# A fused decoder layer on one core: in the compression, work that one engine hands to another is issued further ahead, and a last column changes engine

## The chip, the cores and the metric

The kernel runs on one core of a Trainium2 chip. A core has five engines with a queue of instructions each: TensorE (matmuls, PE in the profile, its weight loads PEld), VectorE (DVE), ScalarE (ACT), GpSimd (POOL) and SyncE (SP, which here issues most DMA transfers). Each engine takes its instructions in the order in which the program issued them; between engines, semaphores make a reader wait for its writer. The metric is the device time of one execution in microseconds, as a median of several runs.

## The reference, cut to what matters

One decoder layer for 320 tokens (256 of a prompt, 8 x 8 of running requests): a SwiGLU feed-forward, a mixer of retention heads and of sparse attention, and a second feed-forward, each with a residual and a LayerNorm. The change lies in one part of the sparse attention, the compression of the cached keys and values of 8 requests of 2048 tokens:

```
chunks = x.reshape(B, n_chunks, 16, 2, 128)
h = einsum('pd,pdf->f', pos_emb, w1)
for r in range(2):
    h = h + einsum('bnskd,sdf->bnkf', chunks, w1r[r])[:, r:r + n_cmp]
return einsum('bnkf,fd->bnkd', gelu(h), w2)
```

It is done once for the keys and once for the values, each with weights of its own: w1 (4096 x 256) and w2 (256 x 128).

## The kernel before, in words

All products are made in a split form: a float32 operand is written as a high half (a rounded copy, ScalarE, line 219) plus a low half (the difference, VectorE, line 220), and `mm3` (lines 213 to 215) issues three matmuls for one product. `split` issues the two halves; the second of the three matmuls is the first that needs the low half of the moving operand.

A generator-based scheduler decides the order in which instructions are issued. The main generator issues a few matmuls, adds their estimated time to a clock, and yields; then `tick` runs one step of each background task that is due (two steps at most). A task yields the time until its next step, or a condition. The scheduler does not reorder a queue: the order of issue is the order on each engine.

The compression (`compress`) goes over 64 rows m, each in two halves (n = 2m and 2m + 1); 8 rows make a pair (two requests; pairs 0 to 3 are keys, 4 to 7 values). A half row has 18 matmuls in three groups of six, with a tick after each group: two groups use the two parts "e" and "o" of the row's chunks, the third uses their sum ("both") with the sum of the two matching weights ("cs"), so that three products do the work of four. At the start of row m:

- `cx_split(m + 2)` splits e and o of the row after next (ScalarE 128x1024, VectorE 128x1024) and then adds them in place (VectorE, line 716);
- `cx_both(m + 1)` splits that sum for the next row (128x512 on each);
- `cx_load` issues page loads from the cache, six of every eight on SP and two on GpSimd. They go into rooms that rows read before have freed.

The split weights of the keys (`cw`, tag G) and their sums (`cs`, on tags wh, wl, K0 and x0) are replaced part by part (k = 0 to 7) by those of the values while pairs 3 and 4 run: a load on SP, a split (`cw_split`), the sum of the two halves of the table on GpSimd (`cw_sum`, line 668), and the split of that sum (`cs_split`). At the start of the stage the last two key sums (k = 6, 7) are made in the same way.

When a pair is done, a background task `cpost` takes its three accumulators over: it combines them (lines 833 to 839), applies position bias and gelu (lines 844, 845, and 815 to 819 in `gelu`), multiplies with w2 on TensorE (tag cw2), for each half f of the hidden width, and writes the result to DRAM (`c_aside`, line 862). The tiles y and u of its work are in the ring of x that the next stage (`w_in_nsa`) needs: the first high half of x (line 539) lies there.

Of the kernel before, what the change touches and what calls it, by code (L numbers as in the profile page):

```python
# [11 lines left out]
AF = mybir.ActivationFunctionType  # L12
# [155 lines left out]
class Builder:  # L168
# [556 lines left out]
    def compress(self):  # L725

        raw = {}

        loads = {}
        for half, first, n in ((2, 0, 16), (3, 2, 8), (5, 6, 8), (4, 10, 16)) + tuple((h, 4 * h - 10, 8) for h in range(6, 16)):  # L730
            for k in range(32 // n):
                loads.setdefault(first + k, []).append((half, n * k, n * k + n))
        for n in range(128):
            m, s2 = divmod(n, 2)
            pair, i = divmod(m, 8)
            if s2 == 0:
                if n == 0:
                    self.rr_rest()
                if m < 62:
                    self.cx_split(m + 2)  # L740
                if m < 63:
                    self.cx_both(m + 1)
                    self.rows_split = m == 62
                for load in loads.get(m, ()):
                    self.cx_load(*load)
            if n in (3, 5, 7, 9):
                k = n // 2 + 3
                room = self.sums_room(k)
                if k > 5:
                    self.cw_sum(room, self.chunk[:, 1024 * (k % 2):1024 * (k % 2) + 1024])  # L750
                self.cs_split(k, room)
            if n in (32, 40):
                raw[n // 8 - 4] = self.cw_load(1, n // 8 - 4)
            if i == 0 and s2 == 0:

                banks = {6: ("x0", "m0", "m3"), 7: ("x2", "x3", "x1")}
                acc = [self.p(t) for t in banks.get(pair, ("x2", "x3", "m1") if pair % 2 else ("x0", "x1", "m0"))]
                if pair == 7:
                    self.free = ["x0"]
            eo, both = self.cx_ring(m)  # L760
            for t in range(3):
                for f in range(2):
                    if t < 2:
                        o = (2 * s2 + 1 - t) * 256 + 128 * f
                        wh, wl = (self.cw[i][:, k, o:o + 128] for k in range(2))
                        hi, lo = (x[:, 512 * s2 + 256 * t:512 * s2 + 256 * t + 256] for x in eo)
                    else:
                        o = s2 * 256 + 128 * f
                        wh, wl = (self.cs[i][k][:, o:o + 128] for k in range(2))
                        hi, lo = (x[:, 256 * s2:256 * s2 + 256] for x in both)  # L770

                    self.mm3(acc[t][:, 256 * f:256 * f + 256], wh, wl, hi, lo, i == 0 and s2 == 0 and f == 0,
                             i == 7 and s2 == 1 and f == 1, 0.11)
                yield
            k, step = divmod(2 * (n - 50), 7)
            if 0 <= k < 8 and step in (0, 1):

                self.cw_split(k, raw[k])
            elif 0 <= k < 8 and step in (2, 3):

                r = raw.pop(k)
                place = r.rearrange("p (s h f) -> p s h f", s=2, h=2)[:, :, 0]
                self.cw_sum(place, r)
                self.cs_split(k, place)
                if k < 6:
                    raw[k + 2] = self.cw_load(1, k + 2)
            if i == 7 and s2 == 1:
                self.posts += 1
                self.spawn(self.cpost(pair, acc), 0.3 if pair < 7 else 10.0)
            if n == 116:  # L790
                self.w_limit, self.ahead = len(self.wq), 0
                self.w_feed()
            if n == 112:

                self.kh, self.kl = 1, 0
                self.x_back(range(0, 12, 2))
                self.x_back([14], self.chunk[:, 0:640].rearrange("p (k t) -> p k t", k=2))
            elif n == 117:
                self.spawn(self.x_scale())
            elif n in (118, 123):  # L800
                self.ahead += 1
                self.w_feed()
        self.compressed = True
# [5 lines left out]
            self.nc.sync.dma_start(out=d, in_=self.x_aside[:, m:m + 2])  # L809
            self.d[m:m + 2] = d[:, 0], d[:, 1]  # L810

    def gelu(self, hs, u, wait=0.0):

        nc = self.nc
        nc.vector.scalar_tensor_tensor(u, u, 1.0 / 0.044715, hs, op0=ALU.add, op1=ALU.mult)
        yield wait
        nc.scalar.activation(u, u, AF.Tanh, scale=0.044715 * math.sqrt(2.0 / math.pi))
        yield wait
        nc.vector.scalar_tensor_tensor(u, u, 1.0, hs, op0=ALU.add, op1=ALU.mult)

    def cpost(self, pair, acc):

        nc = self.nc
        kind, b = pair // 4, 2 * (pair % 4)
        work = self.work[1] if pair < 7 else self.t([128, 1024], "r0")
        y, u = work[:, 0:512], work[:, 512:1024]
        w2 = self.cw2[kind]
        po = (yield from self.hold()) if pair == 7 else self.p("m2")
        rows = y.rearrange("p (m r v) -> p r m v", r=2, v=2)
        two = lambda a: a.rearrange("p (m v) -> p m v", v=2)  # L830
        for f in range(2):
            q, p, c = (a[:, 256 * f:256 * f + 256] for a in acc)
            nc.scalar.activation(u[:, 0:256], q, AF.Copy)
            yield 1.0
            nc.vector.tensor_tensor(rows[:, 1, 0:127], two(p[:, 0:254]), two(u[:, 2:256]), op=ALU.add)
            nc.scalar.activation(rows[:, 1, 127:128], two(p[:, 254:256]), AF.Copy)
            yield 0.6
            nc.vector.tensor_tensor(u[:, 0:256], p, u[:, 0:256], op=ALU.add)
            nc.vector.tensor_tensor(rows[:, 0], two(c), two(u[:, 0:256]), op=ALU.subtract)
            if pair == 7 and f:  # L840
                self.free += ["x2", "x3", "x1"]
            yield 1.5
            pc = self.posc[:, 2 * kind + f:2 * kind + f + 1]
            nc.scalar.activation(u, y, AF.Square, bias=pc)
            nc.scalar.activation(y, y, AF.Identity, bias=pc)
            yield 1.5
            yield from self.gelu(y, u, 1.5)
            yield 5.0 if pair < 7 else 2.5
            if kind == 0:
                self.mm(po, w2[:, f], u, f == 0, f == 1, 0.86)  # L850
            else:
                for k in range(4):
                    g = u[:, 256 * (k // 2):256 * (k // 2) + 256].rearrange("p (n v) -> p n v", v=2)[:, :, k % 2]
                    self.mm(po[:, 128 * k:128 * k + 128], g, w2[:, f], f == 0 and k == 0, f == 1 and k == 3, 0.22)
        if kind == 0:
            nc.scalar.activation(y.rearrange("p (b v n) -> p b n v", b=2, v=2),
                                 po.rearrange("p (b n v) -> p b n v", b=2, v=2), AF.Copy, scale=0.5)
        else:
            nc.scalar.activation(y, po, AF.Copy, scale=0.5)
        if pair == 7:  # L860
            self.drop(po)
        nc.gpsimd.dma_start(out=self.c_aside[:, kind, 256 * b:256 * b + 512], in_=y)
        self.posts -= 1
        if pair == 7:
            self.kc, self.vc = (self.t([128, 8, 256], f"K{k}") for k in range(2))
            for k, t in enumerate((self.kc, self.vc)):
                nc.gpsimd.dma_start(out=t.rearrange("p b c -> p (b c)"), in_=self.c_aside[:, k])
            self.kc = self.kc.rearrange("p b (v n) -> p b v n", v=2)
# [1022 lines left out]
```

## Time and profile before

| | us |
|---|---|
| median of 3 runs | 2881.12 (2876.95 to 2886.17) |
| profiled execution, its own time | 2884.2 |
| its span, first to last instruction | 2882.5 |
| TensorE busy | 2797.6 (97%) |
| VectorE busy | 1553.5 (54%) |
| ScalarE busy | 1202.3 (42%) |
| GpSimd busy | 346.5 (12%) |

The mean granted TensorE clock is 0.991 of full speed. The compression lies between about 950 and 1271 us of the span. A busy TensorE is not one at its peak: matmuls overlap, their ends are modelled, and a short wait can hide under a drawn end. So matmuls in a stretch are counted as well as waits. In a list of instructions, the bracket gives the engine's idle time before the instruction and what ended it.

### The profile page before, as it was taken

The page shows a single profiled execution, that of the slowest core. Times are in us where ns is not written, and L with a number is a line of the kernel's source. Part 1 is how long each engine was busy: PE and PEld are TensorE (multiplying, and loading weights), DVE is VectorE, ACT ScalarE, POOL GpSimd, SP SyncE. Part 2 cuts the span into 40 slices and gives each one's busy share as a digit, 9 for nine tenths or more (in the row PEclk, how much of TensorE's full clock was granted, in tenths as well). Part 3 has the DMA queues.
Part 4 walks back from the last instruction along what each step waited for, and adds up shares of the span by engine and source line. Part 5 has one row for each costly group of instructions (what it writes and reads, how often), then busy time and mean ns, then how long its engine had stood idle before and what let it go on. Part 6 is the DMA issues. An engine that isn't in the chain of part 4 may idle for free. (4 is left out here: it accounts for less than half of the span.)

```text
span 2882.5 us, 49616 instructions
## 1 busy us (share of the span) xinstructions
PE 2797.6 (97%) x19841; PEld 2715.4 (94%) x19841; DVE 1553.5 (54%) x1921; ACT 1202.3 (42%) x1684; POOL 346.5 (12%) x420
## 2 busy tenths in 40 slices
PE   9999999999999998989999999999999999999996
PEld 9999999999999997988888888989999999999996
DVE  4333333357768667684574455673333333366665
ACT  4333333344445455444444445343333333355453
POOL 0000000000102223213232111350000000001111
PEclk9999999999999999999999999999999999999998
DMA  6555444456657444336667664544444444444442
GB/s 225 177 195 177 153 147 153 147 161 199 198 167 235 133 132 137 116 130 239 196 229 252 227 220 164 194 136 154 152 149 150 150 150 150 149 147 151 147 150 92
DMA packets 202600, 484.74 MB, mean 168 GB/s; under 512 B 24257, under 2 KB 100930, under 8 KB 200450
## 3 DMA queue, kind: packets, MB, share of 16 engines
q1 hardware_dynamic: 192546, 451.30, 48.6%
q0 software_dynamic: 9824, 30.29, 3.1%
q8 instruction: 155, 2.54, 0.4%
q14 instruction: 75, 0.61, 0.1%
HBM read 467.47 MB, written 22.28 MB: 170 GB/s over the span
## 5 line engine op out<-in xcount | busy, mean ns | idle before, releaser
L220 DVE TENSOR_TENSOR wl<-raw,wh 128x1024 fp32r<-128x1024 f32 x650 | 816.2, 1256 | 1082.5 <-ACT wh L219 1062.9
L219 ACT ACTIVATE wh<-raw 128x1024 fp32r<-128x1024 f32 x650 | 688.1, 1059 | 1169.6 <-PE m L214 1130.5
L213 PE MATMUL m<-x,wh 128*128 128x320 f32 x3664 | 1150.5, 314 | 12.3 <-ACT wh L219 6.4
L214 PE MATMUL m<-x,wh 128*128 128x320 f32 x3664 | 1134.5, 310 | 4.6 <-DVE x L540 4.6
L215 PE MATMUL m<-x,wl 128*128 128x320 f32 x3664 | 1133.9, 309 | 0.4 <-DVE wl L220 0.4
L213 PEld LDWEIGHTS m<-x,wh 128*128 128x128 f32 x3664 | 692.0, 189 | 36.1 <-issue 22.6
L214 PEld LDWEIGHTS m<-x,wh 128*128 128x128 f32 x3664 | 692.4, 189 | 6.9 <-DVE x L540 6.2
L215 PEld LDWEIGHTS m<-x,wl 128*128 128x128 f32 x3664 | 691.7, 189 | 0.8 <-DVE wl L220 0.8
L213 PE MATMUL m<-r,wh 128*128 128x320 f32 (+1 forms) x1592 | 495.8, 311 | 3.6 <-ACT r L219 1.8
L214 PE MATMUL m<-r,wh 128*128 128x320 f32 (+1 forms) x1592 | 488.3, 307 | 6.6 <-DVE r L220 6.6
L215 PE MATMUL m<-r,wl 128*128 128x320 f32 (+1 forms) x1592 | 490.8, 308 | 0.0
L213 PEld LDWEIGHTS m<-r,wh 128*128 128x128 f32 x1592 | 299.0, 188 | 9.8 <-issue 3.7
L214 PEld LDWEIGHTS m<-r,wh 128*128 128x128 f32 x1592 | 299.4, 188 | 9.3 <-DVE r L220 8.4
L215 PEld LDWEIGHTS m<-r,wl 128*128 128x128 f32 x1592 | 298.2, 187 | 0.0
L476 POOL TENSOR_TENSOR t<-x,x 128x320 f32<-128x320 f32 x3 | 2.7, 914 | 1415.7 <-DVE x L456 719.9
L220 DVE TENSOR_TENSOR r<-G,r 128x640 fp32r<-128x640 f32 (+1 forms) x184 | 156.7, 856 | 0.0
L213 PE MATMUL x<-r,G 128*128 128x256 f32 x480 | 138.6, 289 | 0.0
L214 PE MATMUL x<-r,G 128*128 128x256 f32 x480 | 136.6, 285 | 0.0
L215 PE MATMUL x<-r,G 128*128 128x256 f32 x480 | 136.4, 284 | 0.0
L219 ACT ACTIVATE r<-G 128x640 fp32r<-128x640 f32 (+1 forms) x184 | 130.1, 712 | 0.0
L220 DVE TENSOR_TENSOR r<-x,r 128x1024 fp32r<-128x1024 f32 (+1 forms) x76 | 75.7, 996 | 40.3 <-ACT r L219 40.3
L213 PEld LDWEIGHTS x<-r,G 128*128 128x128 f32 x480 | 92.4, 192 | 1.1 <-issue 1.0
(384 smaller groups left out, 2249.5 us busy)
## 6 DMA issues: line engine op xcount, KB each, us to landing
raw<-wup SPq DMA_DIRECT2D x352, 512.0 KB
raw<-wdn SPq DMA_DIRECT2D x176, 512.0 KB
raw<-win_ret SPq DMA_DIRECT2D x48, 512.0 KB
raw<-win_nsa SPq DMA_DIRECT2D x40, 512.0 KB
raw<-wout SPq DMA_DIRECT2D x32, 512.0 KB
r<-pks SPq DMA_DIRECT2D x96, 128.0 KB
x<-pkc SPq DMA_DIRECT2D x152, 64.0 KB
K<-cw1k SPq DMA_DIRECT2D x16, 512.0 KB
```

The lines of the kernel that those rows point to most:

```text
L213: mm(out, wh, xh, start=start, stop=False)
L214: mm(out, wh, xl, start=False, stop=False)
L215: mm(out, wl, xh, start=False, stop=stop)
L219: self.nc.scalar.activation(hi, src, AF.Copy)
L220: self.nc.vector.tensor_tensor(lo, src, hi.bitcast(F32), op=ALU.subtract)
L476: nc.gpsimd.tensor_tensor(s, self.d[0], self.d[1], op=ALU.add)
```

## The change

Four things change in `compress` and `cpost`; the arithmetic is the same.

1. At the start of a row, `cx_both(m + 1)` is issued before `cx_split(m + 2)`, not after it.
2. The key sums 6 and 7 are made on GpSimd at n = 0 and 2, their splits stay at n = 7 and 9. The parts of the value table come at n = 50, 53, 56, 59, 63, 66, 69, 72 (before: 50, 54, 57, 61, 64, 68, 71, 75); the sum on GpSimd is issued with the split of the part, the split of the sum two half rows later (before: both one half row after the split).
3. In `cpost` the last column of a row block is copied by VectorE instead of ScalarE.
4. The steps of `cpost` and `gelu` get other distances, a post begins only when it is the only one open, and a step is added between the cw2 matmul and what follows.

```diff
+        turns = [50 + 13 * k // 4 for k in range(8)]
...
-                if m < 62:
-                    self.cx_split(m + 2)
                 if m < 63:
                     self.cx_both(m + 1)
                     self.rows_split = m == 62
+                if m < 62:
+                    self.cx_split(m + 2)
...
             if n in (3, 5, 7, 9):
                 k = n // 2 + 3
-                room = self.sums_room(k)
-                if k > 5:
-                    self.cw_sum(room, self.chunk[:, 1024 * (k % 2):1024 * (k % 2) + 1024])
-                self.cs_split(k, room)
+                self.cs_split(k, self.sums_room(k))
+            if n in (0, 2):
+                k = 6 + n // 2
+                self.cw_sum(self.sums_room(k), self.chunk[:, 1024 * (k % 2):1024 * (k % 2) + 1024])
...
-            k, step = divmod(2 * (n - 50), 7)
-            if 0 <= k < 8 and step in (0, 1):
+            if n in turns:
+                k = turns.index(n)
 
                 self.cw_split(k, raw[k])
-            elif 0 <= k < 8 and step in (2, 3):
-                r = raw.pop(k)
-                place = r.rearrange("p (s h f) -> p s h f", s=2, h=2)[:, :, 0]
-                self.cw_sum(place, r)
-                self.cs_split(k, place)
+                place = raw[k].rearrange("p (s h f) -> p s h f", s=2, h=2)[:, :, 0]
+                self.cw_sum(place, raw[k])
+            if n - 2 in turns:
+                k = turns.index(n - 2)
+                self.cs_split(k, raw.pop(k).rearrange("p (s h f) -> p s h f", s=2, h=2)[:, :, 0])
                 if k < 6:
                     raw[k + 2] = self.cw_load(1, k + 2)
...
-    def gelu(self, hs, u, wait=0.0):
+    def gelu(self, hs, u, wait=0.0, then=0.0):
...
         nc.scalar.activation(u, u, AF.Tanh, scale=0.044715 * math.sqrt(2.0 / math.pi))
-        yield wait
+        yield then
...
     def cpost(self, pair, acc):
+        yield lambda: self.posts == 1
...
             nc.vector.tensor_tensor(rows[:, 1, 0:127], two(p[:, 0:254]), two(u[:, 2:256]), op=ALU.add)
-            nc.scalar.activation(rows[:, 1, 127:128], two(p[:, 254:256]), AF.Copy)
-            yield 0.6
+            nc.vector.tensor_copy(rows[:, 1, 127:128], two(p[:, 254:256]))
+            yield 0.4
...
-            yield 1.5
+            yield 2.5 if pair < 7 else 1.5
             pc = self.posc[:, 2 * kind + f:2 * kind + f + 1]
             nc.scalar.activation(u, y, AF.Square, bias=pc)
             nc.scalar.activation(y, y, AF.Identity, bias=pc)
-            yield 1.5
-            yield from self.gelu(y, u, 1.5)
-            yield 5.0 if pair < 7 else 2.5
+            yield 1.0
+            yield from self.gelu(y, u, 2.5 if pair < 7 else 1.5, 1.0)
+            yield 2.0
             if kind == 0:
                 self.mm(po, w2[:, f], u, f == 0, f == 1, 0.86)
...
+            yield 2.0
```

## Rows read from the trace of the kernel before

**Rows 1.** Stretches: us, busy time (instructions) by engine, clock, DMA share, GB/s.

```profile
960.00:1050.00 90.00, 87.75 (x725) 85.51 (x725) 64.17 (x83) 43.33 (x65) 24.46 (x43) 1.00 0.45 128
1050.00:1096.00 46.00, 41.23 (x330) 39.06 (x328) 31.25 (x41) 25.06 (x36) 13.47 (x20) 1.00 0.50 147
1096.00:1160.00 64.00, 52.92 (x377) 49.33 (x378) 45.93 (x57) 32.37 (x47) 20.44 (x30) 0.92 0.44 130
1160.00:1220.00 60.00, 59.37 (x504) 58.97 (x504) 40.03 (x57) 28.98 (x45) 14.84 (x28) 1.00 0.40 117
1220.00:1271.40 51.40, 46.74 (x389) 45.53 (x387) 41.53 (x55) 21.60 (x34) 5.57 (x7) 1.00 0.35 120
```

**Rows 2.** Waits of TensorE, 960 to 1270: us in total, times, longest.

```profile
PE m L214 <- DVE r L220: 8.4, 9, 2.8
PE m L214 <- DVE K L220: 4.5, 6, 1.7
PE m L213 <- ACT x L219: 3.4, 1, 3.4
PE x L214 <- DVE r L220: 2.5, 1, 2.5
PE m L213 <- ACT r L219: 2.4, 2, 1.3
```

**Rows 3.** Waits of ScalarE, 960 to 1270.

```profile
ACT x L836 <- DVE x L835: 41.0, 14, 6.9
...
ACT wl L219 <- POOL K L668: 9.2, 3, 4.1
ACT wh L219 <- POOL K L668: 7.8, 3, 3.0
...
ACT x L219 <- POOL K L668: 5.0, 1, 5.0
...
ACT K L219 <- POOL x L668: 3.7, 1, 3.7
```

**Rows 4.** Timelines of ScalarE, VectorE, TensorE around one stall: start, duration, instruction.

```profile
1011.45 0.17 ACT L836 ACTIVATE x<-x 128x2 f32<-128x2 f32 x1 [2.49 <-DVE x L835]
...
1014.03 1.04 ACT L219 ACTIVATE r<-x 128x1024 fp32r<-128x1024 f32 x1
...
1016.97 0.68 DVE L220 TENSOR_TENSOR K<-x,K 128x512 fp32r<-128x512 f32 x1
...
1017.71 0.39 PE L214 MATMUL m<-K 128*128 128x256 f32 x1 [0.84 <-DVE K L220]
```

**Rows 5.** Groups by shape, 960 to 1270: count, busy us, mean ns, idle before.

```profile
L220 DVE TENSOR_TENSOR r<-x,r 128x1024 fp32r<-128x1024 f32 x41 | 50.2, 1224 | 38.8 <-ACT r L219 38.8
L219 ACT ACTIVATE r<-x 128x1024 fp32r<-128x1024 f32 x41 | 43.2, 1053 | 14.5 <-PE x L215 8.6 <-DMA x<-pkc 2.3 <-PE m L215 2.1
L716 DVE TENSOR_TENSOR x<-x 128x512 f32<-128x512 f32 x41 | 30.3, 739 | 1.4
...
L220 DVE TENSOR_TENSOR r<-x,r 128x512 fp32r<-128x512 f32 x30 | 20.5, 684 | 0.0
L219 ACT ACTIVATE r<-x 128x512 fp32r<-128x512 f32 x30 | 18.6, 619 | 1.7 <-DVE x L716 1.6
```

**Rows 6.** Timelines of VectorE and GpSimd where a weight sum runs.

```profile
1105.56 2.11 DVE L716 TENSOR_TENSOR raw<-raw 128x512 f32<-128x512 f32 x1
...
1105.83 1.28 POOL L668 TENSOR_TENSOR K<-K 128x512 f32<-128x512 f32 x1
```

**Rows 7.** DMA issues: transfers, KB each, median us from issue to landing.

```profile
K<-c_aside POOLq DMA_DIRECT2D x2, 1024.0 KB, 9.7
```

**Rows 8.** Timeline of GpSimd, first page loads of its queue after the stage's start.

```profile
968.12 1.19 POOL L609 DMA_DIRECT2D x<-pkc  x2 [10.89 <-DVE r L220]
```

**Rows 9.** Timelines of ScalarE and TensorE at the end of the compression.

```profile
1274.06 1.01 ACT L539 ACTIVATE x<-x,vecs 128x320 fp32r<-128x320 f32 x2 [1.74 <-DMA c_aside<-x]
...
1274.67 0.42 PE L213 MATMUL m<-x,wh 128*128 128x320 f32 x1 [3.28 <-ACT x L539]
```

## The prediction

> **What bounds the kernel now.** I read the stretches first (busy time of each engine by stage), then who waits for whom, then single stalls in order of time. TensorE is the engine to look at, and the change touches only the compression, so the question is how much TensorE loses there. The yardstick is the stretch from 1160 to 1220 us, in which the second weight table is done and the first post-processing is quiet: 504 matmuls in 60 us, 0.119 us each [rows 1]. At that pace the other four stretches would take 725 x 0.119 = 86.3 of 90 us, 330 x 0.119 = 39.3 of 46, 377 x 0.119 = 44.9 of 64 and 389 x 0.119 = 46.3 of 51.4. So 3.7 + 6.7 + 19.1 + 5.1 = 34.6 us are lost between 960 and 1271 us, more than half of them while the second table is split. The list of waits counts the same loss from the other side: its five largest rows sum to 8.4 + 4.5 + 3.4 + 2.5 + 2.4 = 21.2 us [rows 2], and the granted clock of 0.92 over the 64 us of the worst stretch [rows 1] says that 64 x 0.08 = 5.1 us more went at a lower clock after such gaps. That is 26.3 us, and too little, because a matmul's end is modelled and drawn past the start of the next. The loss lies between 26.3 and 34.6 us; DMA is not in the list at all.
>
> Who makes TensorE wait: the low half of the sums ("both") from VectorE, 8.4 + 4.5 + 2.5 = 15.4 us of the 21.2, and ScalarE for the rest. Neither is busy all the time: ScalarE itself waits, 41.0 us over 14 times for VectorE at the last column (L836) and 9.2 + 7.8 + 5.0 + 3.7 = 25.7 us for GpSimd's weight sums (L668) [rows 3]. One stall shows the mechanism [rows 4]: ScalarE stands at L836 until 1011.45, so the next row's high half begins at 1014.03 only, VectorE comes to the low half of the sums at 1016.97, and TensorE starts its second matmul of the sums at 1017.71, after 0.84 us of waiting for it. An engine with spare time blocks its own queue.
>
> **The change part by part.**
>
> *Sums ahead of e and o.* TensorE needs a row 36 x 0.119 = 4.28 us, and its sums are used after two thirds of the first half, 1.4 us into the row. Counted from the start of row m (when ScalarE may overwrite row m-1), the low half of the sums of row m+1 is due at 4.28 + 1.4 = 5.7 us. Before, VectorE reaches its end at 1.05 (ScalarE, high half) + 1.22 + 0.74 + 0.68 = 3.7 us [rows 5]: 2.0 us to spare, and a ScalarE that starts 1014.03 - 1011.45 = 2.6 us late [rows 4] uses it up. After, the sums need only what the row before left: 0.62 + 0.68 = 1.3 us, 4.4 us to spare. What now comes later is the low half of e and o, by 0.68 us; it is due two rows on, at 8.56 us, and is there at about 3. So this costs nothing, and takes most of the 15.4 us. The page loads that wait for the last low half of a room start some 1.9 us earlier, which can only help.
>
> *The last column on VectorE, posts at a distance.* The 41.0 us of ScalarE waits at L836 go. VectorE pays 14 copies of two columns; between 0.17 us each (the same column on ScalarE [rows 4]) and 0.68 (a whole 512-column pass [rows 5]), so 2.4 to 9.5 us; I take the low end, as it is nearest in size. It gets back its own wait for L836. Squares and tanh go out after later rows' splits, so ScalarE finds their inputs ready. The price could fall on TensorE: its cw2 matmul stands 2.0 instead of 5.0 behind the last gelu step. Counting the scheduler's ticks (one after each 6 matmuls, 0.66 on its clock), the last gelu step is issued at ticks 17 and 40 of a pair and the matmul at ticks 21 and 44, with one row's splits between the two in VectorE's queue only after the gelu step. Behind its row's splits the step ends some 3.7 us into the row, and the matmul comes 5.7 to 6.4 us into it: 2.0 to 2.7 us to spare, so nothing while VectorE is on time, at most 2 us at each of the four in the crowded stretch if it is not. A pair needs 48 ticks, exactly what a pair of rows has; the new wait for one post at a time slips by a tick at most.
>
> *Weight sums.* The sum of a table part now goes to GpSimd with the split and its own split follows two half rows (4.2 us) later, instead of being queued behind it on ScalarE. The sum takes 1.28 us [rows 6] after VectorE's split, so ScalarE's 25.7 us of waits shrink to about nothing; the 3.4 us stall for the seventh split on TensorE goes with them. The next load of the table is now issued 4 half rows ahead of its split instead of 6; some 5 us are left of these after the low half that it waits for. How long it takes to land the trace doesn't show: more than nothing, and less than the 9.7 us of a transfer of twice its size on GpSimd's queue [rows 7], so the split comes 0 to 4.7 us late. That is within the 5.5 us by which the low half of e and o is early, and I take nothing. The two early sums now stand at the front of GpSimd's queue, ahead of page loads, and can start only when the LayerNorm sums have read the tiles that they overwrite. GpSimd sat idle for 10.89 us after those loads [rows 8], so a delay there is absorbed.
>
> *VectorE in the crowded stretch.* Between 1096 and 1160 it was busy for 45.9 us [rows 1] with work that TensorE at full pace does in 44.9. The new spacing (13/4 instead of 7/2 half rows) packs 7% more table parts into it, and more of the sums will now run beside VectorE. Missing: 1 us at least, 6 at most; its lead of 4 us covers some. I take 3 us lost of the 34.6.
>
> *The end.* The last post of the sixth pair now issues its matmul at tick 44, not 47, so ScalarE's copy and the write to DRAM that frees the tile of x come about 2 us earlier against the last matmul. TensorE waited 3.28 us there for L539, which waited 1.74 us for that write [rows 9]. Between 0 and 3.3 us; I take 2.
>
> Sum: 34.6 - 3 + 2 = 33.6 at best, 26.3 - 3 + 2 = 25.3 from the list of waits; I take 30. The stall at the very start of the stage is in code that does not move. The profiled execution took 2884.2 us (span 2882.5), so 2854; it lies 3.1 us above the median of 2881.1, so for a median I say 2851 us.
>
> **Rivals.**
>
> 1. *VectorE becomes the bound while the second table is split.* For it: 45.9 us of work for 44.9 us, and a sum on GpSimd beside it: VectorE's step at 1105.56 took 2.11 us where its kind takes 0.74, with the sum of 1.28 us starting 0.27 us after it [rows 5, 6]. If all eight sums cost 1.4 us each and none is hidden, 11 us go; with the tighter cw2 matmuls (4 x 2) up to 19 are lost. Against it: after that stretch the lead comes back. Gain 12 to 20 us, about 2865. The Trainium skill, page "SBUF — State Buffer", section "Who interferes with whom", says that a GpSimd instruction that reads SBUF and a VectorE instruction with two SBUF inputs share a read port under an exclusive lock, so that the later one waits for the whole of the other; eight sums would then cost at most eight times 1.28 us, 10 us, which alone gives about 2861. The row above agrees with it.
>
> 2. *No change.* The rows of x for the next stage could be what ends last: then a compression that ends earlier only lengthens the 3.28 us wait behind it, and all 30 are given back; 2881. For it: that wait exists. Against it: its releaser is the write behind the last post [rows 9], which moves with the rows, and everything before it is issued by row number.
>
> 3. *Slower: the new order closes a loop in every row.* The sums' high half of a row now stands before the next row's e and o on ScalarE, and needs the in-place sum that VectorE makes after the low half before it. Round the loop: 0.62 + 1.05 + 1.22 + 0.74 = 3.63 us a row [rows 5], against 4.28 that TensorE needs. Today's mean is 311.4 us for 2325 matmuls (the sums of [rows 1]), 4.82 us a row, so the loop would have to come out over 4.82 to lose; at 5.1 it would cost 0.28 x 62 = 17 us: 2898. It needs 1.2 us of locks or waits in each row, and a sum on GpSimd comes only in every third half row of a fifth of the stage.
>
> **How the numbers follow.** Likeliest (0.66): 25 to 37 us gained, 2844 to 2856, predicted 2851. Rival 1 (0.17): 2861 to 2869. Rival 2 (0.11): 2873 to 2888. Rival 3 (0.06): 2889 and up. The range 2843 to 2868 takes in the first two and leaves out somewhat under 2 in 10 and the edges. A difference of 0.3% (8.6 us) is about what a measurement of this kernel can tell from no change; by that, faster 0.83, same 0.11, slower 0.06.
>
> **What would show it.** ScalarE's rows "L836 from L835" and "from POOL L668" are gone; TensorE's waits for the low half of the sums fall from 15.4 us to under 3 between 960 and the end; the granted clock is 1.00 where it was 0.92; the compression ends some 28 us earlier and the wait behind it is 1 to 2 us. Wrong, if VectorE is busy without a gap while the table is split and TensorE waits for it or for L819, or if the wait for L539 grows by what the rows gained.

## The result, and the profile after

| | before | after |
|---|---|---|
| median, us | 2879.96 (4 runs, 2876.95 to 2886.17) | 2848.64 (4 runs, 2847.81 to 2850.41) |
| profiled execution: time, span, us | 2884.2, 2882.5 | 2848.41, 2846.8 |
| mean granted clock | 0.991 | 0.992 |

The ratio is 0.9889, with a 95% interval of 0.9872 to 0.9907: 31.3 us gained, against a forecast of 30 (2851 us as a median). The total was right; its composition was not, as the experiments show.

The first view is that of the stretches (us, busy time and instructions of PE, PEld, DVE, ACT, POOL, granted clock, DMA share, GB/s), for the whole compression before and then for the kernel after, whole and by part.

```profile
949.60:1271.20 321.60, 296.55 (x2364) 286.28 (x2364) 229.87 (x300) 155.72 (x232) 83.32 (x134) 0.98 0.44 129
```

```profile
949.00:1247.00 298.00, 288.28 (x2364) 282.38 (x2364) 233.65 (x314) 160.21 (x219) 87.12 (x138) 0.98 0.48 143
...
960.00:1016.90 56.90, 56.90 (x484) 56.42 (x483) 41.72 (x55) 26.39 (x37) 15.95 (x29) 1.00 0.45 128
1016.90:1025.20 8.30, 2.50 (x7) 1.27 (x6) 4.35 (x5) 3.23 (x5) 0.00 (x0) 0.80 0.35 102
1025.20:1060.00 34.80, 34.80 (x279) 34.32 (x279) 24.40 (x36) 18.14 (x25) 9.10 (x17) 0.95 0.51 153
1060.00:1140.00 80.00, 77.77 (x623) 74.98 (x623) 72.21 (x91) 51.41 (x70) 30.89 (x43) 0.98 0.52 154
1140.00:1190.00 50.00, 50.00 (x427) 50.00 (x426) 37.22 (x53) 26.41 (x36) 13.38 (x25) 1.00 0.47 137
1190.00:1246.90 56.90, 56.90 (x490) 56.90 (x488) 44.55 (x66) 27.89 (x38) 11.57 (x15) 1.00 0.44 145
```

The same 2364 matmuls take 298.0 instead of 321.6 us, 23.6 us less. Most of the stage now runs without a gap at 50 / 427 = 0.117 us a matmul, a little under the 0.119 that the prediction took as its yardstick [rows 1]. At 0.117 us a matmul, an estimate from that stretch, the five stretches of [rows 1] lost 311.4 - 2325 x 0.117 = 39 us, and the six here lose 286.9 - 2310 x 0.117 = 17. Two places carry nearly all that is left: 1016.9 to 1025.2, where TensorE does 7 matmuls, and a shorter one between 1060 and 1140. From 955 to 1240 us the list of TensorE's waits (us, times, longest) has one row; before it had eight, of which [rows 2] shows the five largest:

```profile
PE m L208 <- DVE x L821: 8.0, 2, 5.8
```

No wait for the low half of the sums is left but one of 1.7 us at 951, at the very start of the stage, which both kernels have. ScalarE's waits in the same stretch:

```profile
ACT r L219 <- DVE x L716: 33.1, 26, 2.5
...
ACT r L219 <- DVE raw L716: 16.8, 9, 2.5
ACT K L219 <- DVE x L716: 12.4, 8, 2.1
ACT K L219 <- DVE raw L716: 10.6, 8, 1.7
ACT r L219 <- DMA x<-pkc: 8.5, 1, 8.5
...
ACT wl L219 <- POOL K L668: 4.9, 3, 2.4
...
ACT K L219 <- POOL K L668: 2.4, 1, 2.4
...
ACT wh L219 <- POOL K L668: 0.5, 1, 0.5
```

Against [rows 3]: the 41.0 us at the last column are gone, and the 25.7 us for GpSimd's sums are 4.9 + 2.4 + 0.5 = 7.8. New are 33.1 + 16.8 + 12.4 + 10.6 = 72.9 us for the in-place sum (L716): the loop that rival 3 described. Neither of TensorE's two waits hangs on it: the longer one hangs on a page load, and at the other VectorE has no idle time (both are shown below). Also new is one wait of 8.5 us for a page load. How it becomes TensorE's longest wait is seen in the timelines of ScalarE, VectorE and TensorE:

```profile
1010.16 0.63 ACT L219 ACTIVATE r<-x 128x512 fp32r<-128x512 f32 x1 [0.70 <-DVE x L716]
1019.32 1.06 ACT L219 ACTIVATE r<-x 128x1024 fp32r<-128x1024 f32 x1 [8.52 <-DMA x<-pkc]
1020.28 0.61 ACT L819 ACTIVATE x<-x 128x512 f32<-128x512 f32 x1
```

```profile
1022.27 0.68 DVE L821 SCALAR_TENSOR_TENSOR x<-x 128x512 f32<-128x512 f32 x1
```

```profile
1023.01 1.22 PE L208 MATMUL m<-x,cw2k 128*128 128x512 f32 x1 [5.80 <-DVE x L821]
```

ScalarE stands before the split of a row whose pages have not landed; the tanh (L819) is queued behind it, the last gelu step (L821) behind the tanh, the cw2 matmul behind that. TensorE's row names VectorE, though the cause is a transfer three steps back.

Outside the stage, the two profiled executions differ by 35.7 us in span, so 12.1 us lie elsewhere. The wait behind the last rows is shorter. These are TensorE's waits from 1240 to 1290, beside 3.28 us for L539 before [rows 9]:

```profile
PE m L213 <- ACT x L539: 1.1, 1, 1.1
PE m L214 <- DVE x L540: 1.1, 1, 1.1
```

From the last matmul of the rows to the second of x it is 2.89 us instead of 4.58: 1.7 us. Of the rest, some 3 us lie in the next stage: before, TensorE waits 1.7 us for the last gelu step of pair 7, at 1317, and a clock of 0.93 from 1320 to 1345 takes 1.7 us more; both are absent after. Another 0.8 us lie before the stage, and some 4 us behind a 2.2 us wait for a page of the other attention part that comes and goes between executions of several kernels here. The last 2 us or so are not placed. That page wait is no part of the gain: the profiled execution before lay 4.2 us over its median, the one after 0.2 under.

### The profile page after: what moved, and what is told of

It is laid out like the page before. It is cut to its first block, busy times and chain, and to the rows that moved or that the text cites. A ratio compares the mean times of both kernels' runs of the same rounds, so it can differ in the third digit from the quotient of the medians.

```text
span 2846.8 us, 49623 instructions
## 1 busy us (share of the span) xinstructions
PE 2784.3 (98%) x19841; PEld 2708.5 (95%) x19841; DVE 1555.9 (55%) x1937; ACT 1205.5 (42%) x1668; POOL 351.4 (12%) x420
## 5 line engine op out<-in xcount | busy, mean ns | idle before, releaser
L213 PE MATMUL m<-x,wh 128*128 128x320 f32 x3664 | 1148.6, 313 | 10.1 <-ACT wh L219 6.3
L214 PE MATMUL m<-x,wh 128*128 128x320 f32 x3664 | 1132.9, 309 | 4.3 <-DVE x L540 4.3
L213 PEld LDWEIGHTS m<-x,wh 128*128 128x128 f32 x3664 | 690.6, 188 | 33.3 <-issue 22.0
L214 PEld LDWEIGHTS m<-x,wh 128*128 128x128 f32 x3664 | 690.8, 189 | 6.3 <-DVE x L540 5.6
L213 PE MATMUL m<-r,wh 128*128 128x320 f32 (+1 forms) x1592 | 495.5, 311 | 2.3 <-ACT wh L219 1.0
L214 PE MATMUL m<-r,wh 128*128 128x320 f32 (+1 forms) x1592 | 487.8, 306 | 4.4 <-DVE r L220 4.4
L213 PEld LDWEIGHTS m<-r,wh 128*128 128x128 f32 x1592 | 298.7, 188 | 8.4 <-issue 3.7
L214 PEld LDWEIGHTS m<-r,wh 128*128 128x128 f32 x1592 | 299.3, 188 | 6.7 <-DVE r L220 5.8
L213 PE MATMUL x<-r,G 128*128 128x256 f32 x480 | 137.8, 287 | 0.0
L214 PE MATMUL x<-r,G 128*128 128x256 f32 x480 | 135.7, 283 | 0.0
L220 DVE TENSOR_TENSOR r<-x,r 128x512 fp32r<-128x512 f32 (+1 forms) x76 | 79.2, 1049 | 36.5 <-ACT r L219 35.7
L213 PEld LDWEIGHTS x<-r,G 128*128 128x128 f32 x480 | 91.7, 191 | 1.1 <-issue 1.0
```

The lines of the kernel that those rows point to most:

```text
L213: mm(out, wh, xh, start=start, stop=False)
L214: mm(out, wh, xl, start=False, stop=False)
L220: self.nc.vector.tensor_tensor(lo, src, hi.bitcast(F32), op=ALU.subtract)
```

## The experiments

Medians, and ratios to runs of the kernel before on the same chip; the kernel after has 2848.64 us and 0.9889.

| run | median, us (range) | ratio (95%) |
|---|---|---|
| e1_order | 2876.31 (2874.74 to 2878.74) | 0.9983 (0.9974 to 0.9993) |
| e2_sums | 2867.42 (2863.73 to 2871.98) | 0.9943 (0.9927 to 0.9960) |
| e3_posts | 2862.84 (2860.04 to 2865.26) | 0.9928 (0.9912 to 0.9945) |
| e4_no_order | 2848.93 (2848.06 to 2852.08) | 0.9887 (0.9870 to 0.9903) |
| e5_loads | 2843.57 (2838.69 to 2847.75) | 0.9871 (0.9850 to 0.9891) |
| e6_late_sums | 2852.01 (2847.11 to 2852.31) | 0.9898 (0.9882 to 0.9914) |
| e9_sum_dve | 2848.50 (2847.41 to 2849.17) | 0.9888 (0.9871 to 0.9906) |
| e10_first | 2848.05 (2846.96 to 2849.28) | 0.9887 (0.9869 to 0.9904) |
| e11_both | 2841.35 (2839.93 to 2843.07) | 0.9859 (0.9842 to 0.9877) |
| e12_both_no_order | 2845.46 (2843.72 to 2849.51) | 0.9878 (0.9860 to 0.9896) |
| e13_both_all | 2838.80 (2835.30 to 2845.15) | 0.9852 (0.9831 to 0.9872) |
| e14_dist | 2850.80 (2846.80 to 2852.53) | 0.9890 (0.9872 to 0.9908) |

### Which part carries the gain

The prediction gives the new order of sums and splits most of the 15.4 us that TensorE waits for the sums' low half, out of 21.2 us listed. The rival: it is the freed queue of ScalarE, by the posts and the weight sums, and the order matters little. Three kernels make one part alone; the fourth leaves out the order alone.

**e1_order**: the kernel before with the new order only.

```
+                if m < 63:
+                    self.cx_both(m + 1)
+                    self.rows_split = m == 62
                 if m < 62:
                     self.cx_split(m + 2)
-                if m < 63:
-                    self.cx_both(m + 1)
-                    self.rows_split = m == 62
```

> Before plus the new order of the sums alone (both of row m+1 issued ahead of e and o of row m+2). Theory A (each of the three edits takes away a cause of its own, and most stalls have two causes): the waits for the low half of the sums, 15.4 us of TensorE's list, shrink to under 4; the stalls that ScalarE's waits for GpSimd make (3.4 + 2.4 us) stay; 14 to 20 us gained of the 31. Theory B (ScalarE's blocked queue is the cause, the order of the sums does nothing by itself, since a blocked ScalarE is late for everything): under 6 us gained, and the 41 us that ScalarE waits at the last column stay the source of stalls.

It gained 5.4 us. TensorE's first waits, and one of ScalarE's:

```profile
PE m L213 <- ACT r L219: 4.5, 2, 2.3
...
PE m L214 <- DVE r L220: 1.4, 2, 1.0
```

```profile
ACT x L836 <- DVE x L835: 38.9, 14, 6.1
```

The waits for the low half did fall. But ScalarE still stands at L836 for 38.9 us, and TensorE now waits for the high half, one matmul earlier (L213 for L214). The order mostly moved the stall along the chain.

**e2_sums**: the kernel before with only the weight sums at a distance (`turns`, and the sums of n = 0 and 2).

> Before plus the weight sums at a distance alone (early key sums, value table every 13/4 half rows, sum issued with the split, its own split two half rows later). Theory A: the losses of the stretch in which the value table is split fall by a third to a half, 8 to 13 us gained, and the granted clock there rises from 0.92 to 0.97 or more; the waits for the low half of the sums elsewhere stay. Theory B: as much, 10 to 15, because 25.7 us of ScalarE's waits go.

**e3_posts**: the kernel before with only `gelu` and `cpost` of after.

> Before plus the last column on VectorE and the new distances of the posts alone. Theory A: ScalarE's 41 us at the last column go, and with them the stalls of 0.5 to 1.5 us outside the table's stretch; 8 to 14 us gained. Theory B: 20 us or more, since these 41 us are the largest wait in ScalarE's list.

They gained 14.3 and 18.9 us. Waits of TensorE in e2, then in e3:

```profile
PE m L214 <- DVE r L220: 7.7, 10, 2.4
PE m L214 <- DVE K L220: 5.8, 6, 1.6
```

```profile
PE m L208 <- DVE x L819: 9.1, 2, 4.6
PE m L214 <- DVE r L220: 4.1, 4, 1.7
```

With the weight sums alone the waits for the sums' low half stay; the posts alone remove most of them, in the old order. The wait behind the last rows (3.4 us for L539 in e2, 1.1 in e3) and the 1.7 us of pair 7 in the next stage (there in e1 and e2, gone in e3) also belong to the posts. e3 makes the copy on VectorE and the new distances together, so which of the two carries the 18.9 us isn't shown; nor does e2 separate the early key sums from the spacing of the value table.

**e4_no_order**: the kernel after with the old order of `cx_split` and `cx_both` (e1's diff reversed).

> The changed kernel with the old order of the sums put back. Theory A: with ScalarE free the low half of the sums has 2 us to spare in the old order, so that few stalls come back outside the crowded stretch; 3 to 8 us slower than the changed kernel. Theory B: less than 3 us slower. If instead the order is what carried the gain: 15 us or more slower.

2848.93, equal to after. 14.3 + 18.9 = 33.2 us against e4's 32.8: within the spread of the runs (8 us in e2) the two add up, and the order adds nothing on top. From 955 to 1240 us TensorE in e4 waits for the low half of the sums twice only, 1.7 + 0.4 us, in the old order.

### What is left: the stall at 1017, and the one at 1097

In after, e3 and e4 the cw2 matmul behind the late page begins at 1023.01, 1023.41 and 1022.15 us, in e2 the row's first matmul at 1022.38, whatever was done to the rows before: something at nearly the same time holds them. The candidates are SyncE's issue of the page loads, and GpSimd, which makes the early weight sums ahead of its share of the loads. For the stall at 1097 it is the weight sum that runs beside VectorE's split.

**e5_loads**: in the rooms filled first after the start, GpSimd issues three of eight loads instead of two.

```
-... slice(128 * h, 128 * h + 128), 2 if half > 1 else 0)
+... slice(128 * h, 128 * h + 128), 0 if half < 2 else 3 if half < 6 else 2)
```

> The changed kernel with one more of every eight page loads of rooms 2 to 5 on GpSimd's queue (three instead of two), so that SyncE has 80 instead of 96 to issue before row 16. Theory A (SyncE's issue of page loads, some 0.67 us each without a gap from 951 us on, is a floor in time that the faster rows run into; ScalarE waits 8.5 us for the last of them at 1019 and TensorE 6 us behind it): 16 x 0.67 = 10.7 us earlier, ScalarE's wait for the page goes and TensorE's stall at 1017 to 1025 with it, some 5.8 us and 3.4 us of lost clock: 7 to 9 us faster than the changed kernel, 2840 to 2842. Theory B (the transfers themselves or the room's release are late, not their issue): the wait stays where it is, same as the changed kernel within 2 us.

2843.57, 5 us under after, where 7 to 9 were expected. SyncE's timeline, after and then e5 (start, time for all, count; 64 KB each):

```profile
950.89 32.28 SPq L609 DMA_DIRECT2D x<-pkc  x48
984.20 16.23 SPq L609 DMA_DIRECT2D raw<-pkc  x24
1001.45 27.83 SPq L609 DMA_DIRECT2D x<-pkc  x42
```

```profile
951.08 27.15 SPq L609 DMA_DIRECT2D x<-pkc  x40
979.93 12.92 SPq L609 DMA_DIRECT2D raw<-pkc  x20
994.91 28.28 SPq L609 DMA_DIRECT2D x<-pkc  x38
```

From 951 on, SyncE issues without waiting for anything at 32.28 / 48 = 0.67 us a load. The late row needs the 24 loads that begin at 1001.45; at 0.67 us the last goes out at 1017.5, and ScalarE starts on the row at 1019.32. With 40 + 20 loads before it the room begins at 994.91, after SyncE has waited 1.3 us for it to be released, so its issue is no longer what holds this room. ScalarE has no row that waits for a page, and from 1016.9 to 1025.2 TensorE is busy all the time at a clock of 1.00:

```profile
1016.90:1025.20 8.30, 8.30 (x68) 7.82 (x67) 5.71 (x10) 3.75 (x6) 2.69 (x5) 1.00 0.54 158
```

The Trainium skill, page "DMA: Bandwidth & Descriptors", section "Rules for kernel authors", says that spreading transfers over several issuing engines gives no bandwidth and saves only sequencer issue time. The trace agrees: the DMA engines were 45% busy from 960 to 1016.9 us, and the issue time was the floor.

**e6_late_sums**: the kernel after with the key sums 6 and 7 made where the kernel before makes them (n = 7 and 9, just ahead of their split).

> The changed kernel with the key sums 6 and 7 back at n = 7 and 9. Theory A: they have no part in the late page (SyncE's loads come last, not GpSimd's), so the stall at 1017 us stays and the time is that of the changed kernel within 2 us, perhaps 1 us slower from ScalarE's wait for the sum. Theory B (the two sums in front of GpSimd's page loads make the page late): the stall at 1017 us goes, 5 to 9 us faster.

2852.01, not faster. In its profiled execution, at 2847.83 one of the two shorter ones, TensorE waits 3.61 us, until 1021.07, for the same matmul: some 2 us of the stall are the early sums' at most, and the stall itself is not theirs.

**e9_sum_dve**: the value table's sums go to VectorE, so that none runs beside it on GpSimd.

```
-                self.cw_sum(place, raw[k])
+                t = raw[k].rearrange("p (s h f) -> p s h f", s=2, h=2)
+                self.nc.vector.tensor_tensor(place, t[:, :, 0], t[:, :, 1], op=ALU.add)
```

> The changed kernel with the eight value sums on VectorE instead of GpSimd. VectorE gets 8 x 0.74 = 6 us more to do and no neighbour on GpSimd in that stretch. Theory A (beside a sum VectorE loses about a microsecond each time, so the sum's place makes little difference): the stall at 1097 us stays within a microsecond, the kernel the same within 3 us. Theory B (the neighbour costs VectorE more than the sum itself): VectorE less busy, the stall gone, 3 to 5 us faster. Theory C (VectorE is simply full there): the stall grows by up to 6 us, slower by 3 to 6 us.

2848.50, as after. GpSimd, VectorE, TensorE at the stall, in after:

```profile
1095.02 1.61 POOL L668 TENSOR_TENSOR K<-K 128x512 f32<-128x512 f32 x1 [3.59 <-issue]
```

```profile
1095.39 2.32 DVE L220 TENSOR_TENSOR r<-raw,r 128x1024 fp32r<-128x1024 f32 x1
...
1098.35 0.68 DVE L821 SCALAR_TENSOR_TENSOR x<-x 128x512 f32<-128x512 f32 x1
```

```profile
1099.09 0.70 PE L208 MATMUL m<-x,cw2k 128*128 128x512 f32 x1 [2.16 <-DVE x L821]
```

And VectorE in e9, where L784 is the sum and L822 the gelu step:

```profile
1094.85 0.69 DVE L784 TENSOR_TENSOR K<-K 128x512 f32<-128x512 f32 x1
...
1096.06 1.22 DVE L220 TENSOR_TENSOR r<-raw,r 128x1024 fp32r<-128x1024 f32 x1
...
1097.92 0.69 DVE L822 SCALAR_TENSOR_TENSOR x<-x 128x512 f32<-128x512 f32 x1
```

The split beside the sum takes 2.32 us, 1.10 over its 1.22; without it VectorE pays 0.69 us for the sum itself, and the gelu step begins 0.43 us earlier. VectorE has no idle time from 1087.5 to 1101 us in either. Yet TensorE's wait there, and the stretch behind it, do get shorter in e9:

```profile
PE m L208 <- DVE x L822: 1.2, 1, 1.2
```

```profile
1060.00:1140.00 80.00, 78.44 (x642) 75.66 (x641) 72.48 (x101) 52.54 (x71) 19.82 (x37) 1.00 0.54 160
```

The wait is 1.2 us instead of 2.16, the clock stays at 1.00 where after has 0.98, and 642 matmuls are done instead of 623: 19 x 0.117 = 2.2 us. The lock is real, and a part of that stall is its doing; in the time of an execution a gain of this size doesn't show.

**e10_first**: at the stage's start the low half of the first row's sums is made ahead of the second row's split.

```
 def first_splits(self, i):
-    self.cx_split(i)
     if i:
         self.cx_both(0)
+    self.cx_split(i)
     self.cs_split(i, self.sums_room(i))
```

> The changed kernel with the same order at the very start of the stage: the sums of row 0 split ahead of e and o of row 1. TensorE waits 1.69 us there for the low half of the sums in both kernels. If the order of the two splits is what counts where VectorE starts late, this wait goes: 1.5 to 2 us faster. If VectorE's start (the wait for ScalarE's first halves) is what counts, no change.

2848.05, unchanged. The 1.7 us wait at the start goes. ScalarE, earlier by about 1.1 us (1009.01 for 1010.16), then waits 8.60 us for the page, which comes 1.1 us earlier too: in this execution SyncE began the room's loads at 1000.79, not 1001.45, and the cw2 matmul begins at 1021.94. So it isn't shown that the page takes this gain back. e4 shows it the other way round. Here are after and then e4 up to the stall, and e4 in it, where after does 7 matmuls:

```profile
949.00:1016.90 67.90, 66.21 (x549) 64.90 (x550) 50.81 (x66) 33.14 (x48) 22.08 (x38) 1.00 0.46 133
```

```profile
949.00:1016.90 67.90, 64.52 (x532) 62.96 (x532) 49.08 (x65) 32.14 (x48) 19.95 (x34) 1.00 0.47 133
1016.90:1025.20 8.30, 5.49 (x30) 4.26 (x29) 5.55 (x7) 4.63 (x6) 2.15 (x4) 0.82 0.23 68
```

e4 is 17 matmuls, 2.0 us, behind when the stall begins, and some 5 ahead when it ends: a lead ahead of a floor in time is lost at it.

### Together, and the order once more

**e11_both**: e5 and e10 together. If the page was the floor, e10's gain must now show.

> Three of eight page loads of rooms 2 to 5 on GpSimd, and the sums of row 0 ahead of e and o of row 1. Theory A (the gain at the start was swallowed by the floor of SyncE's page loads): without the floor both gains add: 1.7 us and some of the clock under the 2843.6 of the loads alone, 2839 to 2842. Theory B (they don't add, the start is hidden by something else): 2843 to 2845.

**e12_both_no_order**: e11 with the old order.

> The same with the old order within the rows (e and o of row m+2 ahead of the sums of row m+1). Theory A (with the floor gone nothing hides what the order gives, and its 2.4 us of spare time more count): 2 to 5 us slower than with the new order, with waits for the low half of the sums in the list. Theory B (with ScalarE's queue free the old order has spare time enough everywhere but at the start): the same within 2 us.

e11 takes 2841.35, 2.2 us under e5, with runs of both overlapping, so it isn't shown that e10's gain adds. In e11's trace the 1.7 us wait is replaced by one of 1.9 us: VectorE's low half of the first sums meets one of the early key sums on GpSimd and takes 2.20 us, where it took 0.66 in e10.

```profile
959.84 2.20 DVE L220 TENSOR_TENSOR K<-x,K 128x512 fp32r<-128x512 f32 x1
```

```profile
960.20 1.28 POOL L668 TENSOR_TENSOR x<-K 128x512 f32<-128x512 f32 x1
```

e12 takes 2845.46, 4.1 us more than e11, and their runs do not overlap, though the intervals of their ratios do. TensorE's longest wait in e12, and both kernels from 950 to 970, e11 first:

```profile
PE m L214 <- DVE K L220: 2.7, 1, 2.7
```

```profile
950.00:970.00 20.00, 17.95 (x140) 16.91 (x140) 18.44 (x20) 11.20 (x18) 12.36 (x20) 1.00 0.50 147
```

```profile
950.00:970.00 20.00, 16.15 (x112) 15.10 (x111) 18.06 (x20) 11.40 (x18) 10.81 (x17) 0.91 0.47 135
```

The 28 matmuls that e12 lacks are 3.3 us. So the order is worth some 4 us, most of them at the start of the stage, where VectorE is busy with the LayerNorm's last steps until about 960. In after this was hidden: the page's floor took it back, as e4 showed.

**e13_both_all**: e11 with three of eight loads on GpSimd in all rooms (`3 if half > 1 else 0`).

> As the first, with three of eight page loads on GpSimd in all later rooms too. Theory A (SyncE has room after row 16, 4.0 us of issue in a row of 4.28): no further gain, the same within 2 us. Theory B (SyncE is the floor further on as well): another 2 to 4 us faster.

2838.80, the fastest: 1.5% under before (0.9852, 0.9831 to 0.9872), and all its runs lie under all those of after. Against e11 the runs overlap. Of TensorE's waits in the stage, up to 1236 us, one remains:

```profile
PE m L208 <- DVE x L821: 2.2, 1, 2.2
```

**e14_dist**: e11 with the second cw2 matmul of a pair one unit of the scheduler's clock further behind its gelu step, to remove that wait; the step behind the first one gives the unit up.

```
-            yield 2.0
+            yield 2.0 if f == 0 else 3.0
...
-            yield 2.0
+            yield 1.0 if f == 0 else 2.0
```

> As the first, with the second cw2 matmul of a pair 3.0 instead of 2.0 behind its gelu step, and the step behind the first one 1.0 instead of 2.0. TensorE waits 2.2 us and 0.6 us for L821 at the second matmul while the table is split, and 3.4 us go at the lower clock after it. Theory A (VectorE is up to 3 us late there, so one more on the clock takes a third to a half of the wait): 1 to 3 us faster. Theory B (ScalarE stands for TensorE's first matmul when the second half begins earlier, and passes the delay on): the same or up to 3 us slower.

2850.80: 9.4 us slower than e11. TensorE's wait for L821 grows, and ScalarE stands at the head of its queue again (L849 is the square, L844 the last step of the combining before it):

```profile
PE m L208 <- DVE x L821: 10.3, 6, 4.8
```

```profile
ACT x L849 <- DVE x L844: 22.2, 7, 4.1
```

The ticks of a pair are all in use; a unit given to one distance is taken from the others.

## Why the prediction was right, and where it was not

- *Where the loss was.* Right: 34.6 us by the yardstick, 23.6 recovered in the stage and 1.7 behind it. The stage was forecast to end some 28 us earlier, and ended 24 earlier; that the total still came to 31.3 owes some 3 us to the next stage, which the sum did not have. So the mechanism was right in the main, and that the total missed by only 1.3 us is partly luck. The yardstick was itself a little lossy (0.119 against 0.117), so 39 us were there to be had.
- *"Takes most of the 15.4 us"*, of the sums ahead of e and o. This step failed. Alone it brought 5.4 us, on top of the rest nothing (e4); worth 4 us only once the page and the start are mended (e11 against e12). The arithmetic of spare time was not wrong, but away from the start of the stage the old order's 2.0 us are enough when ScalarE is on time; the 2.6 us by which ScalarE came late [rows 4] were the cause, and the order only a cushion for it.
- *Last column and posts.* The right mechanism, under-sized: I gave the 41.0 us of ScalarE's waits no share of their own in TensorE's loss, and most of TensorE's 15.4 us to the order. e3 makes the posts the largest part, 18.9 us, as the prediction's own stall had shown: "An engine with spare time blocks its own queue." The copy on VectorE (L841, 128x2) costs 0.150 us, 0.17 taken.
- *Weight sums.* ScalarE's waits fell to 7.8 us, not to nothing; alone 14.3 us, more than the 3.4 us stall that I named.
- *The crowded stretch.* Taken as 3 us lost. Measured: one wait of 2.16 us, where a cw2 matmul was said to be tight, and the lower clock behind it (0.98 over 80 us, 1.6 us). The lock of rival 1 is there (2.32 us for 1.22), but VectorE as the bound of the whole stretch is not: e9 takes the lock away and gets some 2 us there.
- *"DMA is not in the list at all."* True of TensorE's waits and wrong as a conclusion: ScalarE's releasers already held 2.3 us for a page load [rows 5], and SyncE already issued at the same rate (48 loads in 31.85 us). With the rows 3% faster that became the longest stall, 5.8 us, with the clock at 0.60 over the 7 us behind it (2.8 us). e5 shows it.
- *The end.* 2 us taken, 1.7 measured.
- *Not foreseen.* Some 3 us in the next stage, of which e3 gives 1.7 to the posts of pair 7. Nor was it foreseen that the early key sums, moved to the stage's start, can meet VectorE there (2.20 us for 0.66 in e11).

Rival 2 is out: the wait behind the rows shrank, as did the time. Rival 3's loop exists, 72.9 us of ScalarE's waits, and TensorE, at full pace in most of the stage, does not feel it; its 3.63 us a row were not measured by themselves. So the sum came out because the loss was measured on TensorE, where it does not matter which edit removes it; the attribution by the name of the last releaser was what misled. Open stay the last wait at 1097, which e9 shortened to 1.2 us and no run removed, and what makes the page wait of the other attention part come and go.

## What to carry to other kernels

Read what ends the bound engine's wait, then what that engine itself stood at before, and go on until an engine is found that waits at the head of its queue with time to spare: mend that, and the orders downstream may stop to matter. Before a stage is sped up, look at the queues that run through it without a pause, a DMA issuer above all: they are the next floor, and a lead gained ahead of them is lost there. Distances in a full schedule are traded against each other, so after moving one look at all the others.

## What the runs showed of the hardware

- SyncE took 0.67 us to issue a 64 KB page load (32.28 us for 48), with the DMA engines at a 0.45 share: a rate of issue, not of bandwidth, for in e5, with more loads beside it on GpSimd, it took 0.68 (27.15 us for 40). Three eighths instead of a quarter of the loads on GpSimd moved the room forward by 6.5 us.
- A VectorE split that started 0.37 us into a GpSimd sum took 2.32 instead of 1.22 us. The Trainium skill, page "SBUF — State Buffer", section "Who interferes with whom", has the later of the two wait for the other's end; 1.61 - 0.37 = 1.24 us of the sum were left, and 1.10 were added, which agrees. Who waits does not always agree: in [rows 6], which the prediction took to agree, VectorE's step is drawn as starting 0.27 us ahead of the sum, and it is VectorE that took 1.37 us longer, while the sum took 1.28; in e11 it started 0.36 us ahead and took 1.5 us longer.
- After TensorE's gap of 5.8 us the matmuls went on at the lower of its two levels, 1.2 GHz, though TensorE had no further gap: the granted clock is 0.50 from 1023 to 1028 and 0.60 from 1023 to 1030, 2.8 us lost.

```profile
1023.00:1028.00 5.00, 4.99 (x17) 3.96 (x18) 3.30 (x4) 2.58 (x4) 0.60 (x2) 0.50 0.32 93
```
